# Stores on GpSimd's queue, the residual in groups of 768 tokens, and early s tiles in a two-layer encoder

## Chip, cores and metric

The kernel runs on one core of a Trainium2 chip. The metric is the device time of one execution in microseconds. Before the change it was 1968.9 us, the median of three runs (1966.53, 1968.9 and 1973.58).

## What is computed

Two requests, 512 tokens (prompt, "p") and 1024 tokens (sample, "s"), go through the same two layers in float32. Layer 0 is multi-head latent attention: x + W_out(attention(RMSNorm(x)) * silu(gate)). Layer 1 is a chunked gated MLP:

```
h = rmsnorm(x, g);  u, v, gate = split(h @ w_in, 3)          # 1024 -> 3 x 2048
u = gelu(u);  v = layernorm(gelu(v), ln_g, ln_b)
sv = einsum('gpq,bnqgd->bnpgd', w_s, chunks_of_128(v)) + b_s  # mixes 128 tokens of a chunk
x + (u * sv * silu(gate)) @ w_out                             # 2048 -> 1024
```

A last RMSNorm follows. Everything that feeds a matmul is written as a high and a low part (hi = the value rounded to the matmul's type, lo = value - hi) and multiplied in three matmuls: hi x hi, hi x lo and lo x hi.

## The kernel before

**Layout.** Features lie on the 128 partitions (8 tiles of 128 for the model's 1024), tokens along the free axis. Attention and the output projections work on blocks of C = 512 tokens: blocks 0 and 1 of the sample, block 2 of the prompt, 1536 tokens in all. The gMLP's input projection works on two groups G of 768 tokens (2H, H = 384), because it multiplies 2 x 2 blocks with seven products in place of eight (`LEFT`, `sums`). For that it needs sums of weight blocks. Those of the v part are made beforehand and kept in DRAM (`w_sums`, Sv), those of u and the gate part in the first group and kept for the second (`bu_src`, Su).

**Stages in order.** Input projection of the sample; its attention; input projection of the prompt (with the first half of the v weight sums woven in); its attention; output projection of the sample (`AOut.out`, two blocks, with the other half of the weight sums) and of the prompt (block 2); then for each group G: `b_v` (v part and its statistics), `b_ug` (16 units, Gelu and Silu alternating, each pair followed by the mix), and output projection `b_out` (block 0 after group 0; blocks 1 and 2 after group 1).

**What goes through DRAM.** The residual x1 after layer 0 (`x1d`, one DRAM tile per 512-token block and feature tile, stored at L751), read by `b_prep` into the hQ tiles (L887 to L898) and again as xr in `b_out` (L1227); v (`v2d`, L1029, read as vin at L1063); s = u * sv * gate (`sd`, L1133, read as s by `s_load`, L1154); the weight sums (L819, L826, L864); y of block 0 (`yd`, L1248); and the output y.

**Queues.** All of these DMAs, loads and stores, are issued from SP, in one order. A DMA in SP's queue waits for what it reads and for the buffer that it writes, and all later DMAs wait behind it. GpSimd (POOL) has only the sums of squares (`sq_acc`, L225 and L1255), the power -0.5 of the norms (`token_pow`, L166) and a few copies.

**What sets the order.** The program is a list of steps in which pieces of one stage are woven by hand between the matmul blocks of another; weights are loaded and split ahead of the step that uses them (`Weights.reach`). The framework's planner then orders each engine's instructions by priority and by its own estimate of when each can run, so a load or split may run well before its place in the list. Each engine carries out its instructions in that order.

**Memory around the last gate unit.** `b_ug` uses the pools h2b (gb, 36 KB per partition) and pu (vin 2 x 6 KB, sv 2 x 3 KB, uo 6 x 3 KB, t). When it ends, both are closed and the pool po with the split s tiles (2 KB each, hi and lo) is opened over the same memory (`open_out`). In group 1, three pairs of s tiles (`npre`) lie in a pool of their own, pre, and are loaded in the last unit; in group 0, none. The raw s tiles come from the ring tmp of five buffers, which all stages share.

**Statistics.** A norm needs sums over all features: squares are summed on POOL, the sum is split (ACT, DVE), multiplied with ones (PE, ps_n), reduced on DVE, raised to -0.5 on POOL, spread as a diagonal (dg, DVE), split again, and multiplied with ones (PE, ps_n). `stats`, `rb0` and `rb1` do it for layer 1, `lat0` to `lat2` for the latents, `half_norm` and `half_scale` for the last block at the end of the program.

Of the kernel before, what the change touches and what calls it, by code (L numbers as in the profile page):

```python
# [22 lines left out]
C = 512  # L23
# [65 lines left out]
def trunk_kernel(tc, A):  # L89
# [142 lines left out]


    def setup():
# [20 lines left out]
        for g in range(3):  # L255
            for k in range(KD):
                st["x1d", g, k] = st["dram"].tile([128, C], F32, name=f"x1_{g}_{k}")
# [475 lines left out]
    class AOut:  # L733
# [9 lines left out]
        def out(self, f, c):  # L743
# [7 lines left out]
            nc.sync.dma_start(out=st["x1d", g, f], in_=x)  # L751
# [58 lines left out]
    def w_sums(u):  # L810

        vu, kt, hf = u // 8, u // 2 % 4, u % 2
        o = slice(hf * 256, hf * 256 + 256)

        def load():
            t = st["wsum", u] = st["ws"].tile([128, 4, 256], F32, tag="ws", bufs=3 - vu, name="ws")
            nc.sync.dma_start(out=t, in_=A["wv"][vu][:, :, kt, o])  # L819

        def make():
# [4 lines left out]
            nc.sync.dma_start(out=st["Sv", vu][:, :, kt, o], in_=t)  # L826
# [18 lines left out]
    def bu_src(G, n, j):  # L845
# [11 lines left out]
        def m1(t, _):  # L857
            x = st["a", n, 1] = t
            o = [st["ws"].tile([128, 1024], F32, tag="su", bufs=4, name="su") for _ in range(2)]
# [3 lines left out]
            for h in range(2):  # L863
                nc.sync.dma_start(out=sd[:, h * 1024:(h + 1) * 1024], in_=o[h])  # L864
# [17 lines left out]
    def b_prep(G):  # L882
# [128 lines left out]
    def b_v(G):  # L1011

        out = []
        for vu in range(2):
# [3 lines left out]
            def sink_of(j, vu=vu):  # L1018
                def sink(fi, th, held, ps):
# [9 lines left out]
                    nc.sync.dma_start(out=st["v2d", G][:, tt, fc * C:(fc + 1) * C], in_=c)  # L1029
# [30 lines left out]
    def b_ug(G, early):  # L1060
# [47 lines left out]
        def new_sv():  # L1108
            return st["pu"].tile([128, 2 * H], F32, tag="sv", bufs=2, name="sv")
# [27 lines left out]
        for p in range(8):  # L1137
# [6 lines left out]
            unit(2 * p + 1, AF.Silu, g, early if p == 7 else ((), (), norm_v(p + 1)))  # L1144
            step(end(p, u, g))

    def s_load(g, d, pre=0):
        def fn():
            x = tmp("s")
            t0 = g * C  # L1150
            while t0 < (g + 1) * C:
                G, o = divmod(t0, 2 * H)
                n = min(2 * H - o, (g + 1) * C - t0)
                nc.sync.dma_start(out=x[:, t0 - g * C:t0 - g * C + n], in_=st["sd", G, d][:, o:o + n])  # L1154
                t0 += n
            hl = [st["pre"].tile([128, C], F32R, name=f"s{e}{d}") if d < pre else
                  st["po"].tile([128, C], F32R, tag="s" + e, bufs=24 if g else 16, name="s" + e)
                  for e in "hl"]
            split(hl[0], hl[1], x)
            st["sf", g, d] = hl  # L1160
        return fn

    def b_out(g, extra, last):
# [24 lines left out]
        def fin4(f):  # L1188
# [3 lines left out]
            nc.sync.dma_start(out=A["y"][f][:, :C], in_=y)  # L1192

        def scale_out(bc, o):
            for f in range(KD):
# [3 lines left out]
                nc.sync.dma_start(out=A["y"][f][:, g * C + o.start:g * C + o.stop], in_=y)  # L1199
# [20 lines left out]
        def out(f, u, key, o):  # L1220
# [14 lines left out]
            if u == 1:  # L1235
# [9 lines left out]
                if n == C:  # L1245
                    sq_acc(st["acc2", g], y, f == 0)
                    if g == 0:
                        nc.sync.dma_start(out=st["yd", f], in_=y)  # L1248
# [29 lines left out]

    def steps(lst):
# [13 lines left out]
    def open_sums():  # L1293
        if ("v2d", 0) not in st:
            b_dram()
        st["ws"] = open_pool("ws", side="right")

    def sums_at(n, us):

        if 0 <= n - 2 < len(us):  # L1300
# [247 lines left out]
```

## Time and profile before

| | |
|---|---|
| median of 3 runs | 1968.9 us |
| profiled execution, its own time | 1964.92 us |
| span from first to last instruction | 1963.1 us |
| mean granted clock of the matmul engine | 0.991 |
| PE, DVE, ACT, POOL busy | 1918.7, 1294.8, 889.9, 140.6 us |
| DMA | 269.42 MB, mean 137 GB/s |

The page gives the busy time of each engine (PE is the matmul engine, PEld its weight load), the share by slices of the span, the chain of work that ended last, and groups of instructions with the idle time in front of them. A clock of 1.00 means that the matmul engine ran at the upper of its two levels all through a stretch. SPq and POOLq stand for the instructions of the queues themselves, issues of DMAs among them.

### The profile page before, as it was taken

How to read it: one execution, taken by the hardware profiler on the slowest of the kernel's cores; microseconds unless marked ns; L12 is line 12 of the kernel's file. 1: busy time of each engine (PE TensorE's matmuls, PEld its weight loads, DVE VectorE, ACT ScalarE, POOL GpSimd, SP SyncE). 2: the span in 40 equal slices, each digit the busy share in tenths (PEclk: the TensorE clock that was granted, in tenths of full speed). 3: DMA queues.
4: the chain of work that ended last, by engine and by line, in shares of the span. 5: the costliest groups of instructions: out<-in, count | busy, mean ns of one | idle time of the engine just before them, and what ended most of it. 6: DMA issues, size and time to landing. Idle time of an engine off the chain costs nothing.

```text
span 1963.1 us, 26564 instructions
## 1 busy us (share of the span) xinstructions
PE 1918.7 (98%) x10226; PEld 1696.1 (86%) x10226; DVE 1294.8 (66%) x1990; ACT 889.9 (45%) x1382; POOL 140.6 (7%) x99
## 2 busy tenths in 40 slices
PE   8999999999998999998999999999999999999998
PEld 6888888888886888886889999988888999998887
DVE  7443777777877787747758777766655665656443
ACT  5322544454543555323544544553444454545321
POOL 5100000000011000122000000001100000000111
PEclk9999999999998999998999999989999999999999
DMA  5211000000126311765557655466575555546443
GB/s 162 86 39 58 27 13 22 17 28 17 38 77 213 107 47 63 235 226 188 183 169 237 199 183 182 157 208 199 160 257 187 190 171 186 165 137 224 167 166 102
DMA packets 127342, 269.42 MB, mean 137 GB/s; under 512 B 12400, under 2 KB 54896, under 8 KB 127216
## 3 DMA queue, kind: packets, MB, share of 16 engines
q1 hardware_dynamic: 127216, 267.73, 42.2%
q8 instruction: 80, 1.31, 0.3%
q14 instruction: 46, 0.38, 0.1%
HBM read 198.74 MB, written 65.01 MB: 134 GB/s over the span
## 4 chain that ended last, share of the span: by engine, by line
PE 85%; DVE 7%; DMA 4%; issue 2%; ACT 1%; POOL 0%; SPq 0%; POOLq 0%; DVEq 0%; ACTq 0%
PE s L595 9%; PE mm L145 7%; PE mm L146 7%; PE mm L147 7%; PE X L984 6%; PE X L985 6%; PE X L986 6%; PE mm L1233 4%; PE mm L1232 4%; PE mm L1234 4%; PE pst L627 3%; PE Z L985 3%; PE Z L984 3%; PE Z L986 3%; PE sv L1118 2%; PE o L146 2%
## 5 line engine op out<-in xcount | busy, mean ns | idle before, releaser
L63 ACT CAST w_hi<-w_raw 128x1024 fp32r<-128x1024 f32 (+3 forms) x267 | 261.0, 978 | 383.2 <-PE mm L146 101.9
L64 DVE TENSOR_TENSOR w_lo<-w_raw,w_hi 128x1024 fp32r<-128x1024 f32 (+3 forms) x267 | 304.5, 1141 | 187.3 <-ACT w_hi L63 186.7
L225 POOL TENSOR_TENSOR acc<-acc,sq 128x512 f32<-128x512 f32 x70 | 115.7, 1654 | 1456.5 <-ACT sq L223 574.8
L1233 PE MATMUL mm<-sl,w_hi 128*128 128x512 f32 (+1 forms) x416 | 157.0, 377 | 2.9 <-DVE sl L151 2.9
L1232 PE MATMUL mm<-sh,w_hi 128*128 128x512 f32 (+1 forms) x416 | 156.3, 376 | 1.9 <-ACT sh L150 1.9
L1234 PE MATMUL mm<-sh,w_lo 128*128 128x512 f32 (+1 forms) x416 | 156.5, 376 | 0.0
L610 ACT ACTIVATE p<-s,sm 128x1024 f32<-128x1024 f32 (+1 forms) x96 | 93.3, 974 | 103.9 <-DVE sm L606 103.8
L150 ACT CAST pth<-pst 128x512 fp32r<-128x512 f32 x160 | 86.5, 591 | 67.2 <-PE pst L627 65.2
L145 PE MATMUL mm<-h_hi,w_hi 128*128 128x512 f32 x288 | 114.8, 399 | 1.0 <-ACT rbc L310 0.9
L147 PE MATMUL mm<-h_hi,w_lo 128*128 128x512 f32 x288 | 113.2, 393 | 0.0
L146 PE MATMUL mm<-h_lo,w_hi 128*128 128x512 f32 x288 | 113.1, 393 | 0.0
L604 DVE TENSOR_REDUCE sm<-s 128x1 f32<-128x1024 f32 (+1 forms) x80 | 97.6, 1220 | 19.5 <-PE s L595 19.4
L151 DVE TENSOR_TENSOR ptl<-pst,pth 128x512 fp32r<-128x512 f32 x160 | 104.7, 683 | 8.4 <-ACT pth L150 8.3
L994 ACT COPY t<-X 128x384 f32<-128x384 f32 (+1 forms) x88 | 44.5, 511 | 126.0 <-PE X L986 125.1
L1233 PEld LDWEIGHTS mm<-sl,w_hi 128*128 128x128 f32 x416 | 79.1, 190 | 18.5 <-DVE sl L151 4.6
L1232 PEld LDWEIGHTS mm<-sh,w_hi 128*128 128x128 f32 x416 | 79.2, 190 | 16.3 <-ACT sh L150 2.2
L1234 PEld LDWEIGHTS mm<-sh,w_lo 128*128 128x128 f32 x416 | 79.2, 190 | 13.9
L146 PE MATMUL o<-ptl,vh 128*128 128x256 f32 x320 | 91.1, 285 | 0.0
L147 PE MATMUL o<-pth,vl 128*128 128x256 f32 x320 | 91.0, 284 | 0.0
L145 PE MATMUL o<-pth,vh 128*128 128x256 f32 x320 | 90.2, 282 | 0.0
L984 PE MATMUL X<-gbh,w_hi 128*128 128x384 f32 x256 | 85.9, 335 | 3.3 <-DVE uo L1083 3.2
L984 PE MATMUL X<-gah,w_hi 128*128 128x384 f32 x256 | 86.9, 339 | 0.0
(292 smaller groups left out, 5112.5 us busy)
## 6 DMA issues: line engine op xcount, KB each, us to landing
w_raw<-wbo SPq DMA_DIRECT2D x50, 512.0 KB, 3.4
w_raw<-wug SPq DMA_DIRECT2D x48, 512.0 KB, 4.4
w_raw<-sv SPq DMA_DIRECT2D x32, 512.0 KB, 3.7
su<-su SPq DMA_DIRECT2D x32, 512.0 KB, 4.1
w_raw<-su SPq DMA_DIRECT2D x32, 512.0 KB, 4.8
w_raw<-wa SPq DMA_DIRECT2D x25, 512.0 KB, 3.6
w_raw<-wv SPq DMA_DIRECT2D x24, 512.0 KB, 3.6
v2d<-c SPq DMA_DIRECT2D x48, 256.0 KB, 2.5
```

Source lines behind the costliest of these rows:

```text
L63: self.nc.scalar.copy(hi[:, :n], raw[:, :n])
L64: self.nc.vector.tensor_tensor(out=lo[:, :n], in0=raw[:, :n], in1=hi[:, :n].bitcast(F32), op=ALU.subtract)
L145: pe.matmul(out, lh, rh, start=(i == 0), stop=False)
L146: pe.matmul(out, lh, rl, start=False, stop=False)
L147: pe.matmul(out, ll, rh, start=False, stop=(i == n - 1))
L595: pe.matmul(s[:, j2 * C:(j2 + 1) * C], l[:, o], r[:, cc], start=(j == 0), stop=(j == 4))
L984: pe.matmul(ps, lh, rh, start=first, stop=False, skip_group_check=True)
L985: pe.matmul(ps, lh, rl, start=False, stop=False, skip_group_check=True)
L986: pe.matmul(ps, ll, rh, start=False, stop=last, skip_group_check=True)
L1232: pe.matmul(ps, wh[:, ksl(kk)], sh, start=(k == 0), stop=False)
L1233: pe.matmul(ps, wh[:, ksl(kk)], sl, start=False, stop=False)
L1234: pe.matmul(ps, wl[:, ksl(kk)], sh, start=False, stop=(k == 15))
```

## The change

Every store to DRAM (x1d, Sv, Su, v2d, sd, yd and y) is issued with `pool_e.dma_start` (new function `store`); SP issues loads, and the few copies within the chip's memories that rotate halves. The residual is kept in DRAM tiles of 768 tokens (one per group and feature tile), so `b_prep` loads a feature tile with one DMA, while block 1 of the output projection stores and reads its residual in two pieces (`by_group`). The weight sums are made in 8 units of [128, 4, 512] in place of 16 of [128, 4, 256], with 2 buffers (first half of them) and 1 (second half) in place of 3 and 2, every second or third weight block. Group 0 gets two pairs of s tiles in the pool pre and group 1 keeps three; all s tiles have fixed places, in an order that puts the next three pairs on the memory of vin and the nine after them on that of gb. Loads of s tiles up to 6 (group 0) or 7 (group 1) stand under the last gate unit and are split after it (`s_raw`, `s_split`). The tile sv has one buffer in place of two, and su three in place of four.

```
+    def store(out, in_):
+        pool_e.dma_start(out=out, in_=in_)
+    def by_group(name, f, t0, n):
+        out, a = [], t0
+        while a < t0 + n:
+            G, o = divmod(a, 2 * H)
+            m = min(2 * H - o, t0 + n - a)
+            out.append((st[name, G, f][:, o:o + m], slice(a - t0, a - t0 + m)))
+            a += m
+        return out
...
-                st["x1d", g, k] = st["dram"].tile([128, C], F32, name=f"x1_{g}_{k}")
+                st["x1d", G, k] = st["dram"].tile([128, 2 * H], F32, name=f"x1_{G}_{k}")
...
-            nc.sync.dma_start(out=st["x1d", g, f], in_=x)
+            for d, o in by_group("x1d", f, g * C, C):
+                store(d, x[:, o])
...
-            t = st["wsum", u] = st["ws"].tile([128, 4, 256], F32, tag="ws", bufs=3 - vu, name="ws")
-            nc.sync.dma_start(out=t, in_=A["wv"][vu][:, :, kt, o])
+            t = st["wsum", u] = st["ws"].tile([128, 4, C], F32, tag="ws", bufs=2 - vu, name="ws")
+            nc.sync.dma_start(out=t, in_=A["wv"][vu][:, :, kt, :])
...
-            nc.sync.dma_start(out=st["Sv", vu][:, :, kt, o], in_=t)
+            store(st["Sv", vu][:, :, kt, :], t)
...
-            o = [st["ws"].tile([128, 1024], F32, tag="su", bufs=4, name="su") for _ in range(2)]
+            o = [st["ws"].tile([128, 1024], F32, tag="su", bufs=3, name="su") for _ in range(2)]
...
-                    t0, t1 = 2 * H * G, 2 * H * (G + 1)
-                    while t0 < t1:
-                        g, o = divmod(t0, C)
-                        h, q = divmod(t0 - 2 * H * G, H)
-                        n = min(C - o, H - q, t1 - t0)
-                        nc.sync.dma_start(out=Q[k][:, j + 2 * h, q:q + n],
-                                          in_=st["x1d", g, k + 4 * j][:, o:o + n])
-                        t0 += n
+                    nc.sync.dma_start(out=Q[k][:, j:j + 3:2, :], in_=st["x1d", G, k + 4 * j].rearrange(
+                        "p (a b) -> p a b", a=2))
...
-            return st["pu"].tile([128, 2 * H], F32, tag="sv", bufs=2, name="sv")
+            return st["pu"].tile([128, 2 * H], F32, tag="sv", bufs=1, name="sv")
...
-                    nc.sync.dma_start(out=st["sd", G, 2 * p + e], in_=u[e])
+                    store(st["sd", G, 2 * p + e], u[e])
...
+    def s_tiles(g, d, pool="po"):
+        i = d if g < 2 else d + 16 if d < 8 else d - 8
+        st["sf", g, d] = [st[pool].tile([128, C], F32R, tag=f"s{e}{i}", bufs=1, name="s" + e) for e in "hl"]
+    def s_raw(g, d):
+        def fn():
+            x = st["sraw", g, d] = tmp("s")
+            for s, o in by_group("sd", d, g * C, C):
+                nc.sync.dma_start(out=x[:, o], in_=s)
+        return fn
+    def s_split(g, d):
+        def fn():
+            if g == 2:
+                s_tiles(g, d)
+            split(*st["sf", g, d], st.pop(("sraw", g, d)))
+        return fn
...
-                nc.sync.dma_start(out=A["y"][f][:, g * C + o.start:g * C + o.stop], in_=y)
+                store(A["y"][f][:, g * C + o.start:g * C + o.stop], y)
...
-                nc.sync.dma_start(out=st["xr", f][:, :n], in_=st["x1d", g, f][:, o])
+                for d, q in by_group("x1d", f, g * C + o.start, n):
+                    nc.sync.dma_start(out=st["xr", f][:, q], in_=d)
...
+    def sums_at(n, u0, every):
+        u, i = divmod(n, every)
+        if i == 0 and 0 <= u < 4:
+            step(w_sums_of[u0 + u][0])
+        u, i = divmod(n - 2, every)
+        if i == 0 and 0 <= u < 4:
+            step(w_sums_of[u0 + u][1])
...
-            sums_at(n, range(8))
+            sums_at(n, 0, 2)
...
-                sums_at(2 * f + c - 3, range(8, 16))
+                sums_at(2 * f + c - 3, 4, 3)
...
+        for d in range(NPRE[G]):
+            s_tiles(G, d, "pre")
...
+        n = NPRE[G]
+        for d in (*range(n + 3, n + 12), *range(n, n + 3), *range(n + 12, 16)):
+            s_tiles(G, d)
...
-        npre = (0, 3)[G]
-        b_ug(G, [s_load(G, d, npre) for d in range(npre)])
+    NPRE = 2, 3
...
+        n = NPRE[G]
+        b_ug(G, [s_load(G, d) for d in range(n)] + [s_raw(G, d) for d in range(n, 6)] + [lambda G=G: (
+            s_raw(G, 6)(), s_raw(G, 7)() if NPRE[G] > 2 else None)])
         step(lambda G=G: open_out(G))
-        for d in range(npre, 8):
-            step(s_load(G, d, npre))
+        for d in range(n, 8):
+            step(s_split(G, d) if d < n + 5 else s_load(G, d))
```

## Rows read from the trace of the kernel before

**Rows 1.** The page, busy us of each engine, share of the span, instructions.

```profile
PE 1918.7 (98%) x10226; PEld 1696.1 (86%) x10226; DVE 1294.8 (66%) x1990; ACT 889.9 (45%) x1382; POOL 140.6 (7%) x99
```

**Rows 2.** Waits of PE: us in total, times, longest us.

```profile
PE ps_n L916 <- ACT sh L150: 7.1, 2, 6.7
PE mm L404 <- ACT h_hi L287: 5.8, 1, 5.8
PE ps_n L179 <- ACT sh L150: 3.8, 2, 2.6
PE mm L1233 <- DVE sl L151: 2.9, 3, 1.3
```

**Rows 3.** Windows: us, busy of PE, PEld, DVE, ACT, POOL, clock, DMA share, GB/s.

```profile
600.00:620.00 20.00, 20.00 (x90) 16.54 (x89) 11.26 (x20) 5.77 (x7) 1.81 (x1) 1.00 0.88 275
620.00:640.00 20.00, 15.18 (x48) 10.70 (x47) 16.68 (x27) 6.95 (x11) 1.02 (x1) 0.74 0.42 140
850.00:880.00 30.00, 30.00 (x134) 24.80 (x133) 10.27 (x15) 9.12 (x12) 10.06 (x8) 1.00 0.56 184
880.00:910.00 30.00, 22.24 (x86) 17.44 (x85) 17.57 (x21) 8.93 (x13) 4.99 (x5) 0.83 0.66 207
1302.65:1316.25 13.60, 8.81 (x19) 5.65 (x19) 9.36 (x13) 6.51 (x11) 0.00 (x0) 0.63 0.83 264
1316.25:1329.85 13.60, 13.60 (x61) 11.25 (x60) 10.54 (x15) 7.99 (x11) 0.00 (x0) 1.00 0.91 288
1760.00:1790.00 30.00, 30.00 (x153) 27.31 (x152) 18.54 (x25) 16.08 (x24) 0.00 (x0) 1.00 0.59 189
```

**Rows 4.** Chain that ended last, 580 to 640: start us, us, what.

```profile
599.88 5.94 DMA ws<-wv
...
613.15 6.16 DMA ws<-wv
```

**Rows 5.** The same chain, 870 to 905.

```profile
874.11 2.03 POOL acc L225
...
880.91 0.32 SPq L751
...
881.28 0.43 SPq L896
...
889.85 4.74 DMA x<-xp
...
897.84 0.70 PE ps_n L917
```

**Rows 6.** The same chain, 1298 to 1320.

```profile
1305.03 0.88 DVE uo L1132
1305.92 5.92 DMA sd<-uo
```

**Rows 7.** Timeline of DVE in 590 to 660, with idle time before and releaser.

```profile
619.40 1.35 DVE L825 TENSOR_TENSOR ws<-ws 128x256 f32<-128x256 f32 x3 [5.18 <-DMA ws<-wv]
```

**Rows 8.** Timeline of SP's queue after 1300 and at the end.

```profile
1308.16 9.91 SPq L1154 DMA_DIRECT2D s<-sd  x10
...
1947.56 13.31 SPq L1199 DMA_DIRECT2D y<-y  x16
```

**Rows 9.** Timeline of DVE at the end.

```profile
1956.61 3.22 DVE L1197 SCALAR_TENSOR_TENSOR y<-y,vec,ps_bc 128x256 f32<-128x256 f32 x8 [1.59 <-PE ps_bc L1216]
```

**Rows 10.** Timeline of POOL at the end.

```profile
1955.10 0.71 POOL L166 TENSOR_TENSOR rstd<-ms,mhalf 128x2 f32<-128x2 f32 x1 [6.74 <-DVE ms L163]
```

**Rows 11.** Groups on POOL: count, busy us, mean ns, idle before.

```profile
L225 POOL TENSOR_TENSOR acc<-acc,sq 128x512 f32<-128x512 f32 x70 | 115.7, 1654 | 1456.5 <-ACT sq L223 574.8 <-ACT acc L223 422.6 <-DMA w_raw<-wbo 292.0
L166 POOL TENSOR_TENSOR rstd<-ms,mhalf 128x4 f32<-128x4 f32 (+1 forms) x16 | 17.1, 1068 | 148.0 <-DVE ms L163 148.0
```

**Rows 12.** DMA issues: count, KB each, median us to landing.

```profile
v2d<-c SPq DMA_DIRECT2D x48, 256.0 KB, 2.5
...
y<-y SPq DMA_DIRECT2D x16, 128.0 KB, 1.8
```

More of the change, by code (lines that the diff above doesn't have):

```diff
@@ L254, in setup @@
         act.copy(st["mhalf"], st["mhalf"])
-        for g in range(3):
+        for G in range(2):
             for k in range(KD):
-                st["x1d", g, k] = st["dram"].tile([128, C], F32, name=f"x1_{g}_{k}")
+                st["x1d", G, k] = st["dram"].tile([128, 2 * H], F32, name=f"x1_{G}_{k}")
     step(setup)
@@ L810, in w_sums @@
     def w_sums(u):
-        vu, kt, hf = u // 8, u // 2 % 4, u % 2
-        o = slice(hf * 256, hf * 256 + 256)
+        vu, kt = divmod(u, 4)
         def load():
-            t = st["wsum", u] = st["ws"].tile([128, 4, 256], F32, tag="ws", bufs=3 - vu, name="ws")
-            nc.sync.dma_start(out=t, in_=A["wv"][vu][:, :, kt, o])
+            t = st["wsum", u] = st["ws"].tile([128, 4, C], F32, tag="ws", bufs=2 - vu, name="ws")
+            nc.sync.dma_start(out=t, in_=A["wv"][vu][:, :, kt, :])
         def make():
@@ L863, in m1 @@
             for h in range(2):
-                nc.sync.dma_start(out=sd[:, h * 1024:(h + 1) * 1024], in_=o[h])
+                store(sd[:, h * 1024:(h + 1) * 1024], o[h])
             st["su", n] = o[1]
@@ L1028, in sink @@
                     dve.bn_stats(out=st["bn", tt][:, fc, :], in_=c)
-                    nc.sync.dma_start(out=st["v2d", G][:, tt, fc * C:(fc + 1) * C], in_=c)
+                    store(st["v2d", G][:, tt, fc * C:(fc + 1) * C], c)
                 return sink
@@ L1143, in b_ug, with s_load @@
                 step(mix(p, u, e))
-            unit(2 * p + 1, AF.Silu, g, early if p == 7 else ((), (), norm_v(p + 1)))
+            unit(2 * p + 1, AF.Silu, g, ((), (), norm_v(p + 1)) if p < 7 else early)
             step(end(p, u, g))
-    def s_load(g, d, pre=0):
+    def s_tiles(g, d, pool="po"):
+        i = d if g < 2 else d + 16 if d < 8 else d - 8
+        st["sf", g, d] = [st[pool].tile([128, C], F32R, tag=f"s{e}{i}", bufs=1, name="s" + e) for e in "hl"]
+    def s_raw(g, d):
         def fn():
[L1149 to L1160, printed above, removed]
+            x = st["sraw", g, d] = tmp("s")
[8 more added lines that the diff above has]
+        return fn
+    def s_load(g, d):
+        def fn():
+            s_raw(g, d)()
+            s_split(g, d)()
         return fn
@@ L1191, in fin4 @@
                                      op0=ALU.mult, op1=ALU.mult)
-            nc.sync.dma_start(out=A["y"][f][:, :C], in_=y)
+            store(A["y"][f][:, :C], y)
         def scale_out(bc, o):
@@ L1247, in out @@
                     if g == 0:
-                        nc.sync.dma_start(out=st["yd", f], in_=y)
+                        store(st["yd", f], y)
                     return
@@ L1276, in b_out @@
         return [fin0, fin1, fin2], [[lambda f=f, fn=fn: fn(f) for f in range(KD)] for fn in (fin3, fin4)]
+    w_sums_of = [w_sums(u) for u in range(8)]
+    def sums_at(n, u0, every):
[5 more added lines that the diff above has]
+            step(w_sums_of[u0 + u][1])
     def steps(lst):
@@ L1293, in open_sums @@
     def open_sums():
-        if ("v2d", 0) not in st:
-            b_dram()
+        b_dram()
         st["ws"] = open_pool("ws", side="right")
-    def sums_at(n, us):
-        if 0 <= n - 2 < len(us):
-            step(w_sums_of[us[n - 2]][1])
-        if 0 <= n < len(us):
-            step(w_sums_of[us[n]][0])
-    w_sums_of = [w_sums(u) for u in range(16)]
     n = 0
@@ L1331, in open_out1 @@
         st["go_pool"] = open_pool("outs1")
-        open_sums()
+        st["ws"] = open_pool("ws", side="right")
     step(open_out1)
@@ L1340, in trunk_kernel @@
                 step(lambda f=f, c=c: out_s.out(f, c), ("wao", f))
-                sums_at(2 * f + c - 3, range(8, 16))
-                if 2 * f + c == 13:
+                sums_at(2 * f + c - 3, 4, 3)
+                if 2 * f + c == 14:
                     step(lambda: close_pool("ws"))
@@ L1377, in open_b, with open_in @@
         st["ps"], st["mm"] = open_pool("psumb", space=bass.MemoryType.PSUM), "y"
-    def open_in():
+    def open_in(G):
         st["pre"] = open_pool("pre")
+        for d in range(NPRE[G]):
+            s_tiles(G, d, "pre")
         st["h2b"] = open_pool("h2b")
@@ L1413, in trunk_kernel @@
     for G in range(2):
-        step(open_in)
+        step(lambda G=G: open_in(G))
         for i, s in enumerate(b_v(G)):
```

## Prediction

> **What bounds the kernel now.** I read the page first: the matmul engine is busy for 98% of the span [rows 1], so only the missing 2% and the stretches at a lower clock can be won. Then the waits of PE: beside the start-up (h_hi, 5.8 us, untouched) the long ones are for operands that ACT and DVE split: at ps_n L916, ps_n L179 and mm L1233 [rows 2]. Third, windows around these three places [rows 3]. They show that a wait of a few us costs more than itself, since the granted clock falls to the mean 0.74, 0.83 and 0.63 of its upper level (towards the lower of 1.2 and 2.4 GHz) after PE stood idle. Matmuls begun against an undisturbed neighbour of the same kind give the whole loss:
>
> - Place A, input projection of the prompt: 48 in 620 to 640 against 90 in 600 to 620, so 42 x 20/90 = 9.3 us.
> - Place B, output projection before the gMLP: 86 in 880 to 910 against 134 in 850 to 880, so 48 x 30/134 = 10.7 us.
> - Place C, first output projection of the gMLP: 19 in 13.6 us against 61, so 42 x 13.6/61 = 9.4 us.
>
> Together 29.4 us. Elsewhere PE waits for no transfer, so loads that come earlier can win nothing there. Last I followed the chain of waits through the three places, to see what ends last in each.
>
> **C: s tiles in own memory.** The chain runs over the gate product L1132 at 1305.03, then 5.92 us of the store sd<-uo, then the cast of sl [rows 6]. That cast needs no byte of this store: it writes memory that the stored tile still holds. Ten s loads are issued behind it, from 1308.16 on [rows 8]. The change takes both causes away. Tiles 0 and 1 lie in their own pool and can be split under the last gate unit; 2 to 4 take the 12 KB of the two vin buffers (free after the last mix), 5 to 13 the 36 KB of h2b; only 14 and 15 reach the uo buffers, and they are wanted a third of a projection later. Loads no longer stand behind the stores. The second group of the same kernel has three such tiles already, and from 1760 to 1790, over the same passage, PE is busy for 30.00 of 30 us at full clock [rows 3]. What is late next: the casts of tile 5 on, behind the gate product on DVE (ends 1305.9) while PE finishes the old unit at 1302.65, where the window of rows 3 begins; PE can use tiles 0 to 4 meanwhile (15 matmuls per output block at 13.6/61 = 0.22 us, 3.3 us, and the planner can take a second block). I leave 1 us for it: -8.4 us, bounds 0 (no tile gets free earlier) and -9.4.
>
> **B: residual by 768 tokens, stores off SP.** The chain here is one queue: the x store of SP waits for DVE's sum and goes at 880.91, the hQ loads come behind it from 881.28 on (24 issues in all, 0.43 us each, one every 0.47), then x<-xp goes at 889.85 and takes 4.74; only then can DVE do its sum and, behind it in DVE's order, the dg, sh, sl of the statistics for which PE waits until 897.84 [rows 5]. After the change 8 issues stand where 24 did: 16 x 0.47 = 7.5 us less of SP, and no store in front of them. The last of these loads must still wait for a residual store that now goes through POOL in two pieces. The bytes stay: 3.1 MB of hQ at the 207 GB/s of this stretch [rows 3] is 15 us, at the 288 of the fuller one 11 us. If they start near 876.5, x<-xp lands near 889, not 894.6, and ps_n is fed 5.6 us earlier, at 892.2. PE's idle time of 7.8 us in 880 to 910 [rows 3] ends at 897.84, so PE arrives near 890.1 and would wait 2.1 us. I leave 2.7 us of the loss, with a little at the lower clock: 10.7 - 2.7 = -8.0 us, bounds 0 and -10.7.
>
> POOL is on this chain as well: at 874.11 an acc sum frees the buffer into which x<-xp goes [rows 5]. Two store issues now come in front of that sum, 2 x 1.07 = 2.1 us later (price below); that is covered by the 5.6 us and is why I don't take the full 10.7.
>
> **A: eight weight-sum units of 1 MB instead of sixteen of 0.5 MB.** The chain is made of ws<-wv loads (5.94 and 6.16 us are two of them) [rows 4]; DVE stands 5.18 us in front of a ws sum [rows 7], and the statistics that PE needs queue behind it. The new schedule moves the same bytes; each load has two weight blocks of PE work before it is summed, as before, but twice the size. For it: 2 KB rows instead of 1 KB, no store ahead of a load in SP, 32 DVE sums instead of 64. Against it: two buffers of double size, the next load waits for a store landing that POOL has to issue. In the second set of sums there is a single buffer; SP waits with it for sum and store, with weight and x loads behind, but 3 steps are planned per unit where one was. I take half of the loss, -4.6 us, bounds -9.3 and, if one more stall of this kind arises instead, +9.3.
>
> **The stores on POOL.** 192 stores change queue (v2d 48, the smallest y ones 16, [rows 12] has these two of eight kinds; x1d grows from 24 to 32, sv falls from 16 to 8). No row shows an issue from POOL. From below: SP needs 0.32 us for an x store [rows 5]. From above: the longest POOL pass in the chain takes 2.03 us [rows 5], the mean of its 512-wide sums is 1.65, that of its smallest arithmetic, 4 elements wide, 1.07 [rows 11]. An issue has no data to go through, so I take 1.07: 205 us more on an engine that is busy for 141 of 1963 [rows 1]. Where it lies beside PE it costs nothing; POOL is in order, so what queues behind a store are acc sums and the pow of a norm. Only the end has no cover: eight y stores from 1947.56 [rows 8], then the pow at 1955.10 [rows 10], then eight sums on DVE from 1956.61 [rows 9], each followed by a store that lands after 1.8 us [rows 12]. With p us per issue, the first eight and the last acc sum (0.7) free POOL at 1948.3 + 8p, so the pow is 8p - 6.8 late; the last eight begin near 1957.1 and the end would be 1958.9 + 8p against 1963.1, so 8p - 4.2 more. Both: 16p - 11, at 1.07 +6.1 us; at 0.32 nothing, at 2.03 +21.5.
>
> The Trainium skill, "DMA: Bandwidth & Descriptors", table of specifications, gives about 1 us to the first byte of a DMA issued from GpSimd and 0.6 us for one from SP; the end would by this be +5.0. No run here shows it yet.
>
> **Small parts.** The halved sv buffer: DVE alone writes and reads it, one operation after the other, so no hand-over between engines is added, and PE has no gap to fill there (153 matmuls in 1760 to 1790, busy 30.00 [rows 3]): 0. Three su buffers for four: a unit takes two and its store has a unit's time to land: 0, at worst one landing of a store per unit on DVE. Eight more xr loads: under matmuls, 0.
>
> **Sum.** -8.4 - 8.0 - 4.6 + 6.1 = -14.9 us against the profiled execution's 1964.92 (span 1963.1 and 1.8 around it): 1950.0. The three runs have their median 4.0 higher, at 1968.9, so I add half of that: 1952 us.
>
> **Rivals.**
> 1. *All three places clear*: -9.4 - 10.7 - 9.3 + 6.1 = -23.3, 1943.6 (here and below with the same 2 us). For it: all three hang on SP's order in the chain. Against: at A the load itself is the time.
> 2. *Transfers are the bound, not their order*: A and B stay, C goes. -8.4 + 6.1 = -2.3, 1964.6. For it: DMA's busy share is 0.88 in 600 to 620 and 0.91 after 1316 [rows 3], and neither the bytes at A nor those at B shrink. Against: the share is 0.66 at B, and 8 us of hQ issues in rows 5 are time of the queue, not of the transfers; so I keep it behind the forecast. The Trainium skill, "DMA: Bandwidth & Descriptors", section on issuing engines not being separate queues, says that all issuers run on the same 16 DMA engines and that a second one only saves the sequencer's time. By that rule alone this rival would be the likeliest.
> 3. *The change doesn't do what it says at C*: the planner puts the early splits late, or the store still holds the memory. A and B as in the forecast: -12.6 + 6.1 = -6.5, 1960.4. Against: the second group.
> 4. *Slower: POOL's queue takes over SP's*. Place: the last 16 stores and the pow between them. Price 16p - 11; the wins of 21.0 are used up at p = 2.0 us, and at 2.3, with A unchanged (wins 16.4), it is +25.8 - 16.4 = +9.4, 1976. For it: passes of 2.03 us on this engine, pow and acc behind stores that wait for DVE. Against: POOL's passes over 4 elements are at 1.07.
>
> **How the numbers follow.** Forecast 0.40, rival 1 0.22, rival 2 0.18, rival 3 0.08, rival 4 0.12. About 0.3% (5.9 us) is what can be told from no change; that lies between 1963.0 and 1974.8. Faster: 0.38 of the forecast, all of rival 1, a third of rival 2, 0.05 of rival 3: 0.71. Same: the rest of these three and 0.02 of rival 4: 0.17. Slower: 0.12. The range runs from rival 1 with a free end (1964.9 - 29.4, 1936) to just above rival 2 (1970); rival 4's case lies outside. The forecast's own range is 1943 to 1960.
>
> **What would show it.** C: no wait at L1232 or L1233, clock at 1.0 from 1290 on, s casts before the unit ends. B: hQ as 8 issues, the wait at L916 under 3 us. A: DVE's wait for ws<-wv under 2 us. End: the time from the last wbo matmul to the end longer by about 6 us, and stores on POOL near 1.07 us each. The prediction is wrong if a POOL issue takes over 2 us, or if new waits of PE for a pow or a late load appear where none is now.

## The result, and the profile after

The changed kernel takes 1981.8 us (median of 4 runs, 1978.9 to 1982.9) against 1968.7 for the kernel before (median of 4 runs beside it, 1966.5 to 1973.6): a ratio of 1.0061, 95% interval 1.0039 to 1.0082 (the ratio comes from all runs and is not the quotient of the two medians, here and below). The forecast was 1952, with a range from 1936 to 1970; it is 30 us off and on the wrong side. The profiled execution takes 1978.91 us, its span is 1977.1 (before: 1964.92 and 1963.1), so 14.0 us are to be found.

The busy line of the page, against [rows 1]: PE works as long as before (1919.3 and 1918.7), so the 14 us are idle time. POOL has 192 instructions more, for 102 us.

```profile
PE 1919.3 (97%) x10226; PEld 1696.7 (86%) x10226; DVE 1290.9 (65%) x1958; ACT 888.3 (45%) x1382; POOL 242.8 (12%) x291
```

Waits of PE, against [rows 2] (us in total, times, longest). ps_n L923 and mm L1248 are the lines L916 and L1232 of before (there 7.1 and 1.9 us, with 2.9 at L1233): both waits are still there. The waits at X, Y and Z, in the gate units, are 9.0 us together; before, PE waited 3.2 us at X, 0.4 at Z and not at Y.

```profile
PE mm L418 <- ACT h_hi L301: 5.7, 1, 5.7
PE ps_n L179 <- ACT sh L150: 5.2, 3, 2.8
PE ps_n L923 <- ACT sh L150: 4.3, 2, 3.3
PE mm L1248 <- ACT sh L150: 4.0, 1, 4.0
PE Z L991 <- ACT t L1001: 3.9, 3, 1.5
PE X L991 <- DVE uo L1090: 3.8, 4, 3.2
...
PE Y L991 <- DVE sv L1127: 1.3, 3, 0.6
```

Windows, columns as in [rows 3]: place A (48 matmuls before, 51 now), place B (86 and 97 in this window, but 134 and 125 in the 30 us ahead of it), place C (the stall has moved from the first to the second of two windows). The clock falls at all three as it did.

```profile
620.00:640.00 20.00, 14.65 (x51) 10.76 (x50) 16.90 (x26) 7.51 (x11) 1.75 (x2) 0.83 0.58 199
850.00:880.00 30.00, 28.61 (x125) 23.12 (x124) 13.12 (x18) 8.35 (x12) 14.43 (x17) 1.00 0.69 236
880.00:910.00 30.00, 24.12 (x97) 19.17 (x96) 18.69 (x21) 9.59 (x14) 9.33 (x11) 0.89 0.70 234
1302.00:1316.00 14.00, 13.49 (x66) 11.54 (x64) 8.62 (x12) 7.08 (x11) 1.09 (x2) 1.00 0.64 211
1316.00:1330.00 14.00, 10.55 (x35) 8.49 (x36) 10.98 (x15) 8.18 (x13) 0.00 (x0) 0.76 0.87 291
```

**Where the 14 us are.** A window of fixed times drifts against the work, so I matched the k-th execution of each statement by which ACT or DVE takes a matmul result, in both traces, and took the median delay at the borders of the stages. What the delay grows by in each stage is in the table (us; negative is gained; mid is 960 to 1080, g0 the gate units of group 0 from 1080 to 1300, C 1300 to 1380, m2 up to 1500, g1 the gate units of group 1 up to 1640, where the delay then stays; end is what lies behind the last output matmuls). The other rows are the experiments below, each against the same profiled execution of before. Each row rests on one execution, and those of the kernel before alone lie between 1962.4 and 1974.4 us, so an entry of 1 or 2 us says little unless it recurs in kernels that have the edit in common.

```
                 start    A     B   mid    g0     C    m2    g1   end   span
changed            0.1  -0.8   0.4  -1.2   5.1  -2.7  -1.0   5.9   8.2  +14.0
e1_queue_only      0.7   2.6  -0.8  -1.3   7.6   0.2  -1.0   8.2   1.9  +18.2
e2_rest_on_sp      0.5  -1.2   6.3  -1.1   0.7  -1.7   2.7   0.4   0.4   +7.0
e3_y_on_sp        -0.1   0.0   0.4  -1.2   5.9  -2.8  -1.0   8.1   0.7  +10.0
e4_two_sv          0.4  -1.8   2.0  -1.2   8.7   0.3  -1.0   7.3   8.2  +22.9
e5_sd_on_sp        0.7   0.0   2.4  -1.2   6.9  -3.2  -1.0   2.5   6.3  +13.3
e6_sd_y_on_sp      0.2  -0.9   1.5  -1.3   5.4  -2.5  -1.0   0.5   0.2   +2.1
e7_su_v2d_on_sp    0.4  -1.1   0.3  -0.4   1.0  -3.1  -1.0   7.6   2.6   +6.2
e13_su_on_sp       0.5  -1.4   0.8   2.5   1.3  -2.9  -1.0   8.6   6.1  +14.6
e10_x1_sv_pool     0.5  -1.1   0.6   0.0   1.9  -2.3   0.0   1.6   0.7   +1.9
e9_one_raw_more    0.0  -0.1   0.2  -0.3   0.3  -7.8   0.5   1.6   0.6   -5.0
e11_hq_in_four     0.0  -0.9  -4.1  -0.9   1.1  -2.8   0.2   2.7   0.2   -4.5
e12_both           0.5  -0.5  -2.3  -0.8   1.0  -7.8  -0.3   2.8   0.2   -7.3
e14_two_at_a       0.6  -9.1  12.0  -0.8   0.3  -7.9   1.1   1.6   0.6   -1.5
e15_x1_only        0.2   0.2  -1.6  -1.1   0.3  -0.9   0.1   0.8   0.2   -1.7
```

So the three places gave 3.1 us where 21.0 were forecast, and 19.2 were lost at the gate units and at the end.

**Place A.** The chain there runs over the store of a sum from POOL and then the load into the same buffer:

```profile
599.98 5.09 DMA sv<-ws
605.09 8.04 DMA ws<-wv
```

**The end.** The issues on POOL are cheap, the pow stands behind none of them (rows of its timeline: start, duration, [idle before <- releaser]), against [rows 10]:

```profile
1960.89 0.71 POOL L166 TENSOR_TENSOR rstd<-ms,mhalf 128x2 f32<-128x2 f32 x1 [2.50 <-DVE ms L163]
1963.18 4.31 POOL L234 DMA_DIRECT2D y<-y  x8 [1.58 <-DVE y L1212]
```

The eight end at 1967.49 and the last lands at 1969.10. But the span ends at 1977.1, 8.0 us after the last landing (before: 0.9), and no engine works between. The rows of the program's last line (shortest/median/longest ns, from first start to last end; first the kernel before) name it: a DRAIN of POOL's queue, 9594 ns long, with the last issues in it; before, the longest took 811 ns, with the pow in it.

```profile
L1543 POOLq DRAIN  x3: 34/78/811, 1955.1 to 1962.9; - x3
...
L1569 POOLq DRAIN  x3: 45/102/9594, 1966.7 to 1976.8; - x3
```

**Place B.** The chain is the same with fewer pieces, against [rows 5]: eight hQ issues from 878.35 on, then x<-xp, which now takes 7.91 us (4.74 before) and lands at 892.50.

```profile
884.59 7.91 DMA x<-xp
892.62 0.12 DVE x L764
```

The 9 matmuls lost in the window ahead come from a new stall at 873, where PE waits 1.2 us at ps_n L179. The chain runs there over a store of x from POOL and the x load that waits for its buffer:

```profile
859.63 6.46 DMA x<-x
...
866.22 3.19 DMA x<-xs
```

Between 780 and 920, PE waits at ps_n L179 in every kernel that has the 1 MB weight sums (0.8 to 6.0 us, 13.4 in e14) and in none of the three with sixteen smaller ones (before, e1, e15). From e12 to e14, where two more of these units stand there, the wait grows from 2.8 to 13.4. So the sums of place A have a part in this loss; what the residual's stores in two pieces add was not tried.

**Place C.** The chain, against [rows 6]: no store any more, but the load of an s tile. SP's timeline shows why it starts so late.

```profile
1309.47 1.31 DVE sl L151 x3
1310.77 7.99 DMA s<-sd
1318.78 0.63 ACT sh L150
```

```profile
1309.50 1.19 SPq L904 DMA_DIRECT2D hQ<-x  x2
1310.77 9.70 SPq L1162 DMA_DIRECT2D s<-sd  x6
```

ACT cast five tiles from 1307.62 on; the next cast is that of tile 7. Tiles 0 to 6 were loaded early; the load of tile 7 waited for a raw buffer of the ring of five, so for a split, and went behind two hQ loads of 384 KB. ACT's next cast shows that the wait for a load was there before, too (first line: before, second: changed):

```profile
1313.60 3.41 ACT L150 CAST sh<-s 128x512 fp32r<-128x512 f32 x5 [6.86 <-DMA s<-sd]
...
1318.78 0.62 ACT L150 CAST sh<-s 128x512 fp32r<-128x512 f32 x1 [8.47 <-DMA s<-sd]
```

**Gate units.** ACT's timeline in group 0: two casts of early s tiles stand in ACT's order ahead of copies of t, and wait for their loads.

```profile
1087.95 0.62 ACT L150 CAST sh<-s 128x512 fp32r<-128x512 f32 x1 [2.52 <-DMA s<-sd]
...
1094.69 0.62 ACT L150 CAST sh<-s 128x512 fp32r<-128x512 f32 x1 [4.80 <-DMA s<-sd]
```

And the waits of SP's queue from 1075 to 1190: four loads of s stood at its head until the store of the same data had landed, up to 10.3 us, with the weight loads behind them.

```profile
SPq L55 <- DVE w_lo L64: 44.0, 12, 8.7
SPq L1162 <- DMA sd<-uo: 39.3, 4, 10.3
SPq L1070 <- PE sv L1125: 19.1, 3, 6.4
```

Before, stores of su stood between an sd store and the s load behind it, and the load had nothing left to wait for. SP's timeline of before:

```profile
1082.75 1.19 SPq L1133 DMA_DIRECT2D sd<-uo  x2
1085.36 0.32 SPq L864 DMA_DIRECT2D su<-su  x1
1086.42 0.33 SPq L55 DMA_DIRECT2D w_raw<-wug  x1
1087.63 0.32 SPq L864 DMA_DIRECT2D su<-su  x1
1088.04 1.56 SPq L1154 DMA_DIRECT2D s<-sd  x2
```

In group 1, from 1510 to 1650, s loads stand at the head of SP's queue for an sd store twice as long as before (first line: before):

```profile
SPq L1154 <- DMA sd<-uo: 8.0, 3, 2.8
...
SPq L1162 <- DMA sd<-uo: 17.2, 6, 3.8
```

### The profile page after: what moved, and what is told of

The parts are those of the page before. It is cut to its first block, busy times and chain, and to the rows that moved or that the text cites. A ratio compares the mean times of both kernels' runs of the same rounds, so it can differ in the third digit from the quotient of the medians.

```text
span 1977.1 us, 26633 instructions
## 1 busy us (share of the span) xinstructions
PE 1919.3 (97%) x10226; PEld 1696.7 (86%) x10226; DVE 1290.9 (65%) x1958; ACT 888.3 (45%) x1382; POOL 242.8 (12%) x291
## 4 chain that ended last, share of the span: by engine, by line
PE 72%; issue 9%; DVE 8%; DMA 6%; POOL 2%; ACT 2%; SPq 0%; POOLq 0%; DVEq 0%; ACTq 0%
PE s L609 9%; PE mm L145 6%; PE mm L146 5%; PE mm L147 5%; PE X L991 4%; PE X L992 4%; PE X L993 4%; PE mm L1248 4%; PE mm L1249 4%; PE mm L1250 4%; PE pst L641 3%; PE Z L991 2%; PE Z L992 2%; PE Z L993 2%; PE o L146 2%
## 5 line engine op out<-in xcount | busy, mean ns | idle before, releaser
L1248 PE MATMUL mm<-sh,w_hi 128*128 128x512 f32 (+1 forms) x416 | 155.6, 376 | 4.0 <-ACT sh L150 4.0
L1248 PEld LDWEIGHTS mm<-sh,w_hi 128*128 128x128 f32 x416 | 78.9, 190 | 18.2 <-ACT sh L150 4.4
```

The costliest lines, as they stand in the source:

```text
L1248: pe.matmul(ps, wh[:, ksl(kk)], sh, start=(k == 0), stop=False)
```

## Experiments

### The queue, or the rest of the change

**e1_queue_only** (from before) and **e2_rest_on_sp** (from changed):

```
 e1: all eight kinds of store
-                nc.sync.dma_start(out=st["x1d", g, f], in_=x)
+                pool_e.dma_start(out=st["x1d", g, f], in_=x)
...
 e2: def store(out, in_):
-        pool_e.dma_start(out=out, in_=in_)
+        nc.sync.dma_start(out=out, in_=in_)
```

> The kernel before with its 192 stores issued from POOL, nothing else changed. Theory Q (the queue costs: about 8 us between the last matmul and the end, where POOL's closing DRAIN lasts 9.6 us in the changed kernel, and some us in the gate units because stores land later and the loads of the same data behind them): 1976 to 1981, DRAIN near 9.6 us, last ps_bc to end near 15.4 us instead of 7.3. Rival M (the slowdown comes from the rearranged memory and order: single sv buffer, early s loads, larger weight-sum units; the queue only lengthens what POOL would do anyway): within 3 us of the kernel before, 1966 to 1972.

> The changed kernel with all stores back on SP: residual by 768 tokens, 1 MB weight sums, one sv buffer, early s tiles remain. Theory Q: the end is short again (7 to 8 us after the last ps_bc), place C clears at least as far as with POOL, 1962 to 1968, not slower than before. Rival M: the rearrangement itself loses, and SP now has the stores again, 1972 to 1980.

e1: 1981.0 us, ratio 1.0066 (1.0052 to 1.0079): the queue alone costs all of it, 13 us. Theory Q held for the time, but not for its parts: the end lost 1.9 us, not 8, and the gate units 15.8. e2: 1971.4, ratio 1.0017 (1.0008 to 1.0026): the rest of the change loses too, some 3 us, where Q had expected a gain: place B loses 6.3 us (PE waits 6.0 us at ps_n L179 there) and m2 2.7. With the stores of x1d, Sv and yd on POOL (e10) B loses 0.6; which of the three kinds does it was not tried. Rival M, that the rearranged memory loses, is out for g0, g1 and the end.

### The end

**e3_y_on_sp**, and **e8_pool_ops** (st["pad"] is a column beside the constants):

```
 e3: scale_out, and the same in fin4
-                store(A["y"][f][:, g * C + o.start:g * C + o.stop], y)
+                nc.sync.dma_start(out=A["y"][f][:, g * C + o.start:g * C + o.stop], in_=y)
 e8: setup
         act.copy(st["mhalf"], st["mhalf"])
+        for _ in range(13):
+            pool_e.memset(st["pad"], 0.0)
```

> The changed kernel with only the y stores (24 of 192) on SP; the last store from POOL is then that of sd or yd, long before the end. Theory Q1 (the closing DRAIN waits for what POOL's last stores leave behind): DRAIN under 1 us, 1973 to 1975. Rival Q2 (the DRAIN lasts its 9.6 us whenever POOL has issued any store, but may start earlier, beside the last matmuls, and is hidden): also 1973 to 1975, with a long DRAIN row that ends before the last y lands. Rival Q3 (it starts at the end of the program and lasts 9.6 us however old the last store is): 1980 to 1983 as in the changed kernel.

> The changed kernel with 13 more memsets of one column on POOL at the start (POOL then has as many instruction records, 551, as the kernel before with the queue alone, whose closing DRAIN ended 0.9 us after the last landing; in the changed kernel it ended 7.2 us after). Theory I (the 6.2 us are a fetch of POOL's next instructions, which depends on where its program is cut): DRAIN about 3.3 us, 1975 to 1977. Rival R (they are work that POOL's DMA queue leaves behind): DRAIN 9.6 us, 1980 to 1983.

e3: 1974.5, ratio 1.0030 (1.0018 to 1.0042), 32 stores moved (the expectation said 24). Q2 was right: the DRAIN is still long though POOL's last store (sd) ended 177 us earlier, but it begins with the last pow (1964.4) and is over before the last y lands. Its row:

```profile
L1569 POOLq DRAIN  x3: 40/93/6962, 1964.4 to 1972.8; - x3
```

e8: 1992.0, ratio 1.0131 (1.0109 to 1.0154), the DRAIN at 9.58 us, as in the changed kernel: theory I, as it was put there, is out (though the trace has 549 of POOL's records, not the 551 that were aimed at), and R not shown by that alone. That the kernel got 10 us slower was expected by neither theory (below).

### The gate units

```
 e4_two_sv:        tag="sv", bufs=1 -> 2;  NPRE = 2, 3 -> 1, 3
 e5_sd_on_sp:      store(st["sd", G, 2 * p + e], u[e])  -> nc.sync.dma_start(...)
 e6_sd_y_on_sp:    e5 and e3
 e7_su_v2d_on_sp:  store(sd[...], o[h]) and store(st["v2d", G][...], c)  -> nc.sync.dma_start(...)
 e13_su_on_sp:     store(sd[...], o[h])  -> nc.sync.dma_start(...)
```

> The changed kernel with two sv buffers again, and one early s tile pair in the first group where there are two (memory). Theory S (the single sv buffer delays the gate units: PE waits 1.3 us at Y for sv, and what queues behind): these waits go, the 5 us lost between 1085 and 1180 shrink to 2 or less, and part of the 6 us between 1520 and 1620, total 1974 to 1978. Rival L (the gate units lose because stores from POOL land later and casts of s and loads of v stand behind them): waits for sv go, but the stretch loses the same, 1980 to 1983.

> The changed kernel with only the 32 sd stores on SP. Theory F (with these stores off SP the planner lets the loads s<-sd go to the head of SP's queue, where they wait up to 11 us for a store to land, and the gate units' weights wait behind them): the 5.3 us lost between 1080 and 1180 and the 5.9 between 1520 and 1620 shrink to under 2 each, total 1971 to 1975, SP's waits of s loads for DMA sd<-uo in 1075 to 1190 fall from 39 us to under 10. Rival U (the 32 su stores or the v2d stores are what lands late): the losses stay, 1979 to 1983.

> The changed kernel with the sd and the y stores on SP; x1d, sv, su, v2d and yd remain on POOL. If theory F and the cost of the closing DRAIN are right and add: 1964 to 1968, with places A and B as in the changed kernel and C 2 to 3 us better than before; faster than before by 1 to 4 us. Rival U: 1972 to 1976.

> The changed kernel with the su and v2d stores (80) on SP, sd on POOL. Theory F: SP is busier, but the s loads still wait for stores that land late; the losses of the gate units stay at half or more, 1977 to 1982. Rival U: they go, 1970 to 1974.

> The changed kernel with only the 32 su stores on SP (v2d stays on POOL). Theory S (the su stores stood in SP's queue between an sd store and the s load behind it, and the weight loads kept their places): the 5 us lost between 1080 and 1180 go, the 6 us of group 1 stay, 1974 to 1978. Rival V (the v2d stores): the 5 us stay, 1979 to 1983. DRAIN, if it lasts longer with each store issued from POOL (9.6, 7.0, 4.3 us with 192, 160, 128 in five kernels): about 7 us with these 160; if it follows something else, any value.

- e4: 1987.3, ratio 1.0095 (1.0081 to 1.0109). Theory S is out: with two buffers PE waits at Y for sv 3.9 us instead of 1.3, and e1, which has two as well, shows 4.0. (This kernel loads one s tile twice, 33 s loads for 32, so part of the added time may be its own.)
- e5: 1975.0, ratio 1.0046 (1.0031 to 1.0061); its profiled execution is a long one, at 1978.2. g1 falls from 5.9 to 2.5, g0 does not (6.9), though SP's waits of s loads fell to 3.8 us. So theory F holds for group 1 and not for group 0.
- e6: 1970.7, ratio 1.0014 (1.0002 to 1.0027): g1 and the end together are gone (0.5 and 0.2), g0 stays at 5.4; the expected gain over before did not come.
- e7: 1971.4, ratio 1.0026 (1.0014 to 1.0038): here g0 falls to 1.0 and g1 stays at 7.6. Rival U is right for group 0. ACT waits for no s load from 1075 to 1190 any more, and the wait of 39.3 us is 5.5:

```profile
SPq L1070 <- PE sv L1125: 19.0, 3, 6.3
SPq L1162 <- DMA sd<-uo: 5.5, 2, 5.3
```

- e13: 1979.6, ratio 1.0069 (1.0050 to 1.0088), above the 1974 to 1978 of theory S: the total does not bear it out. In g0 the loss is 1.3 instead of 5.1, but 2.5 us are lost just ahead of it, so that mid and g0 together lose 3.8 us, as in the changed kernel (3.9). There DVE waits 3.7 us for a v2d store from POOL to land, which still holds the memory of uo, and PE waits 2.5 us for DVE. With v2d on SP too (e7) this is not there, and the two stages lose 0.6.

What is shown: the sd stores off SP cost group 1 (e5, e6), and those of su and v2d together cost group 0 (e7); that su alone does it is not shown. In group 1 the wait from above goes with the loss: from 1510 to 1650 it is 16.0 to 17.2 us in the kernels with sd on POOL (changed, e1, e3, e4, e7, e13), and 7.3 to 10.8 in before and in all with sd on SP. For group 0 the way is read from the waits (s loads at the head of SP's queue) and not isolated. The casts in ACT's order are not needed for it: in e1, with 7.6 us lost, SP waits 34.2 us for sd stores, but ACT waits for no s load. And in e5 SP's waits are gone and the loss is not; there SP stood 11.0 us with a vin load for PE, with the weight loads behind that, and ACT still waited 5.0 us for s loads.

### The three places

**e10_x1_sv_pool** is e6 and e7 together. On top of it, **e9_one_raw_more** and **e11_hq_in_four**, and both in **e12_both**:

```
 e9: open_in, s_raw
+            for d in (5, 6):
+                st["rawp", d] = st["pre"].tile([128, C], F32, name=f"rawp{d}")
-            x = st["sraw", g, d] = tmp("s")
+            x = st["sraw", g, d] = st["rawp", d] if g == 0 and d in (5, 6) else tmp("s")
-    NPRE = 2, 3
+    NPRE = 1, 3
-            step(s_split(G, d) if d < n + 5 else s_load(G, d))
+            step(s_split(G, d) if d < 7 + G else s_load(G, d))
 e11: load() of b_prep takes ks, and hQ is loaded pair by pair
-    woven = [[lambda: out_s.stats(1), head[0]], head[1:3], head[3:5]] + ...
+    woven = [[lambda: out_s.stats(1), lambda ld=head[0]: ld((0,))], [lambda ld=head[0]: ld((1,))] + head[1:3], ...
```

> The changed kernel with the sd, su, v2d and y stores on SP; only the residual (32), sv (8) and yd (8) stores remain on POOL. Theory Q (the loss of the changed kernel is the su stores off SP in group 0, the sd stores off SP in group 1, and the closing DRAIN, and these add): group 0 and group 1 lose under 1 us each, C keeps its 2 to 3 us, A and B as in the changed kernel, 1962 to 1966, ratio 0.997 to 1.000. Rival: with the gate stores back on SP the waits come back elsewhere (as with all stores on SP, 6 us at B and 3 us after C): 1968 to 1972.

> The kernel e10_x1_sv_pool with one early s tile in group 0 instead of two, and the 4 KB freed used as raw buffers for tiles 5 and 6, so that tiles 0 to 7 (all that the first three half blocks of matmuls read) are loaded under the gate units, where seven were. Theory R (place C waits because the ring of five raw buffers keeps tile 7's load behind the splits, at 1310.8 us, and its landing behind the hQ loads): PE's wait of 4.0 us for sh at the output projection is under 1 us, the clock stays near 1.0, C gains 3 to 6 us more than in e10, 1957 to 1962. Rival T (the transfers after the unit are the bound, whatever is loaded before): the wait moves to the next tile with the same length, within 1 us of e10.

> The kernel e10_x1_sv_pool with the eight hQ loads of group 0 in four pairs, one per block of the output projection, so that the second x load of the prompt stands behind two of them in SP's queue, not behind eight. Theory O (place B is the order of transfers: the x load takes 7.9 us because 3.1 MB of hQ are ahead of it): the x load takes 3 to 4 us, PE's wait at ps_n L923 falls under 1.5 us, B gains 3 to 7 us, 1957 to 1962. Rival T (the bytes must come in any case, PE then waits for hQ): a wait of about the same length appears at the first matmuls that need hQ or at the casts gah, within 1.5 us of e10.

> The edits of e9_one_raw_more and e11_hq_in_four together. If both theories R and O hold and add: 1953 to 1958, 5 to 8 us faster than the kernel before per the ratio 0.994 to 0.997. If neither: as e10.

e10: 1967.2, ratio 1.0002 (0.9992 to 1.0011). The losses of the queue are gone (g0 1.9, g1 1.6, end 0.7); what is left of the change is worth nothing that the total shows. This is above the 1962 to 1966 of theory Q, and g0 and g1 lose more than the 1 us that it allowed, so the parts add only roughly.

e9: 1962.0, ratio 0.9968 (0.9956 to 0.9980), 5 us below e10. Theory R was right: one more tile loaded in time, and C gains 7.8 us instead of 2.3, almost what the prediction wanted from the whole step. The clock stays up in both windows, where e10 has 0.94 and 0.82:

```profile
1302.00:1316.00 14.00, 12.84 (x57) 10.11 (x56) 9.81 (x13) 6.26 (x11) 0.00 (x0) 1.00 0.84 278
1316.00:1330.00 14.00, 14.00 (x64) 11.58 (x63) 12.54 (x17) 8.37 (x12) 0.00 (x0) 1.00 0.83 275
```

The transfers are no thinner than in e10 (shares 0.84 and 0.83 against 0.80), so the bytes are not what stalled PE.

e11: 1962.9, ratio 0.9976 (0.9965 to 0.9986). Theory O was right: the same bytes, two hQ loads ahead of x<-xp instead of eight, and B gains 4.1 us, though the total is 0.9 us above what O expected. The window of B, against 0.89 with 97 matmuls above:

```profile
880.00:910.00 30.00, 28.34 (x126) 23.28 (x125) 23.09 (x26) 12.56 (x17) 11.23 (x13) 1.00 0.75 265
```

SP's timeline shows the order now:

```profile
878.34 0.33 SPq L760 DMA_DIRECT2D x<-xp  x1
878.76 1.19 SPq L904 DMA_DIRECT2D hQ<-x  x2
880.06 0.54 SPq L760 DMA_DIRECT2D x<-xp  x1
880.65 1.18 SPq L904 DMA_DIRECT2D hQ<-x  x2
```

e12: 1957.3, ratio 0.9946 (0.9933 to 0.9959): faster than both kernels. The gains add, but for 2 us at B.

**e14_two_at_a** and **e15_x1_only**:

```
 e14: (from e12) two of the first four weight-sum units go to the second set
-                sums_at(2 * f + c - 3, 4, 3)
+                sums_at(2 * f + c - 3, 2, 2)
...
 e15: (from before)
-            nc.sync.dma_start(out=st["x1d", g, f], in_=x)
+            pool_e.dma_start(out=st["x1d", g, f], in_=x)
```

> The kernel e12_both with two of the four weight-sum units of place A moved to the second set (six units there instead of four, one buffer). Theory L (place A waits because the third and fourth 1 MB load can only start when the first two sums are stored, and land at full transfers 8 us later, with the statistics behind their sums in DVE's order): DVE's wait of 6.5 us for ws and PE's waits of 3.5 and 2.5 us between 610 and 640 go, A gains 5 to 9 us; what the second set loses with six units is seen apart, between 800 and 880, 0 to 8 us. Rival G (the statistics there are a chain of their own, without cover from PE): A gains under 2 us.

> The kernel before with only its 24 residual stores issued from POOL. If the order on SP at place B is what costs there, these stores alone give little: PE's wait at ps_n L916 stays 5 to 7 us, total 1965 to 1970, no difference. If the store ahead of the hQ loads was the cause: the wait falls under 3 us, 1960 to 1963. DRAIN, if it grows with the number of stores since the start: 2 to 3 us in all, hidden; if it is the same whenever POOL has stored: 7 to 9 us.

e14: 1963.8, ratio 0.9977 (0.9967 to 0.9987). Theory L was right for A: 9.1 us gained, 88 matmuls where e12 has 50, DVE's wait for ws from 6.5 to 2.8 us.

```profile
620.00:640.00 20.00, 19.91 (x88) 16.11 (x87) 17.01 (x26) 11.54 (x19) 1.01 (x1) 1.00 0.22 75
```

The work only moved: B, with six units in the second set, now loses 12.0 us, and 14.3 against e12, more than the 8 expected (PE waits 13.4 us at ps_n L179, 9.7 of them at once).

e15: 1966.7, ratio 0.9989 (0.9980 to 0.9998). The x stores alone, off SP, take PE's longest wait at ps_n L916 from 6.7 to 4.7 us, between the two expectations, and the total hardly changes; so the store ahead of hQ was at most a part of the cause at B.

## Why the prediction was wrong

- **What bounds the kernel** was right as far as it could be tried: C holds 7.8 us (e9), A 9.1 (e14, which loses more than that at B), B at least 4.1 (e11). The change reached little of it.
- **C, -8.4, got -2.7.** The failed step is "what is late next": it took five tiles as what PE lives on and left 1 us. Late next was tile 7, the first that does not fit the ring of five raw buffers, its load behind two hQ loads. The store that I followed in the chain was only one of two waits of about one length: before, DVE's splits waited for it until 1311.94, and ACT's casts for a load until 1313.60.
- **B, -8.0, got +0.4.** The queue as the cause was right, its sizes were not. The failed step is "x<-xp lands near 889", 12.5 us after the hQ loads start at 876.5. They started at 878.35, and x<-xp landed 14.15 us later, at 892.50: inside the 11 to 15 us that I had worked out for the 3.1 MB ahead of it, which are the same whatever the number of issues. Eight issues took 6.13 us, 0.77 each, not 0.47. So x landed 2.1 us earlier than before, not 5.6. That window gained 11 matmuls, 2.5 us, and the window ahead lost 9, 2.0 us, to the stall at ps_n L179, which had no term. What moves B is the place of x<-xp in the queue (e11).
- **A, -4.6, got -0.8.** Fewer, larger loads changed nothing: the third 1 MB load still starts when the first sum is stored and takes 8.04 us. I had named this wait against the change, and half of the loss was a guess. The stall that I put in the bounds, in the second set of sums, came too, in the window ahead of B. Rival 2 had A and B nearly right; it had C wrong, and its 1964.6 lacks what follows.
- **The end, +6.1, got +8.2** by another way. An issue on POOL takes 0.546 us for a y store, not 1.07, so 16p - 11 was below nothing and the queue held up no pow; rival 4's sign came true, but not its place. Of the 8.2 us, 7.1 are what the DRAIN adds behind the last landing; no row of before could tell its length with stores behind it. The +5.0 beside my price put the time to the first byte in place of p; a y store holds POOL for 0.546 us and lands 2.2 us after its issue, against 1.8 from SP.
- **"Where it lies beside PE it costs nothing", got +11.0.** This is the costliest step. I priced POOL's time and asked what queues behind a store on POOL. It had to be asked what the stores had held apart on SP: they stood between loads, and without them loads of s came to the head of the queue and waited there for stores to land, with the weight loads behind them. That the stores' queue costs this is shown; the way is supported by the waits in group 1 and open in part in group 0. The sign of being wrong that I had written down, new waits of PE for a late load, is what came.
- **sv with one buffer: 0.** PE does wait for sv, 1.3 us, but not for lack of the buffer (e4). The +0.1, -1.2 and -1.0 of the start and the stages between were not forecast.
- Sum: -0.8 + 0.4 - 2.7 + 5.1 + 5.9 + 8.2 - 2.1 = 14.0. The interval of 1.0039 to 1.0082 is 7.7 to 16.1 us. (In the chances, the parts of "same" add up to 0.19 and not 0.17, and "slower" is 0.10.)

The rule that I weighed, the Trainium skill's "DMA: Bandwidth & Descriptors", section on issuing engines not being separate queues, spoke for rival 2, and the run with only the issuer changed agrees at A and B: e1 loses 2.6 us and gains 0.8 there. The same page, in its table of issuing engines by pattern, gives plain loads and stores to SP's path; here all 192 stores off it cost 13 us (e1), by the order on SP and the end, while the 48 of e10 cost nothing that its total shows.

## What to carry to other kernels

Before stores leave a queue, look at what they separate there: here a load behind a store was in time only because something stood between, and a load that reached the head early blocked all loads behind it. When a wait is taken away, name the next tile that comes late by its buffer: count the ring. Here the queue got faster by the order of its transfers (4.1 us at B), not by fewer issues of the same bytes.

## What the hardware showed that I had not expected

**POOL's closing DRAIN** gets long with the stores issued from POOL and needs no recent one (in e10 the last is some 556 us old): 2.80 us with 24 stores (e15), 4.76 with 48 (e10), 3.52 with 112 (e7), 4.35 with 128 (e6), 6.96, 6.90 and 6.98 with 160 (e3, e5, e13), 9.59, 9.58 and 9.58 with 192 (changed, e4, e8). Among these it goes by their number and not by their bytes: the three with 160 each lack another kind. From 24 to 48 and from 128 to 192 this is 0.08 us for each store; between 48 and 112 something starts over, and so it must in e1, with 3.32 us for 192. What, was not tried. In the three kernels with 9.6 us, and in no other, one packet of 8 KB of the page's kind "instruction" moves during the DRAIN (at 1970.57 in the changed kernel), so a fetch of instructions is not ruled out as a part of it, though 32 stores more at 0.08 us already make up the step from 160 to 192. The DRAIN is hidden where POOL's last work ends some us before the last y lands. The row of e15:

```profile
L1543 POOLq DRAIN  x3: 40/93/2796, 1953.2 to 1961.1; - x3
```

**A column of padding** (e8) slowed matmuls at a clock of 1.00. In the last projections, with PE busy all the time, the rows of 1800 to 1850 have 216 of them in e8 (first) and 223 in the changed kernel, and the delay grows by 4 us from 1740 to 1940. It is not only there: at 400 us e8 is 3.9 us behind the kernel before, the changed kernel 0.2. The 13 memsets run at the start of the program; what else differs is that all tiles behind the column lie further on in memory. That it is the address was not tried.

```profile
1800.00:1850.00 50.00, 50.00 (x216) 40.13 (x216) 30.39 (x33) 23.52 (x34) 6.74 (x4) 1.00 0.62 210
```

```profile
1800.00:1850.00 50.00, 50.00 (x223) 41.39 (x222) 25.29 (x27) 18.75 (x26) 8.38 (x5) 1.00 0.58 200
```
